# VectorE's and ScalarE's orders written out by name in a hybrid convolution, SSD and FFN block

## The chip, the cores and the metric

The kernel runs on one core of one Trainium2 chip. The metric is device time in microseconds of one execution. Three runs of the kernel before took 1012.22 to 1015.75 us, median 1013.33. A further execution was profiled.

## What is computed

The reference is one block over 512 tokens of width 1024, in float32. Cut to what matters:

```
h = rms_norm(x); proj = h @ w_in          # val | glu | z | x, B, C | dt | gates
conv = silu(layer_norm(conv31(val * sigmoid(glu)))) @ conv_pw   # 31 taps per channel
ssm  = per group of 4 heads: conv4 + silu of x, B, C; chunked scan with
       decay = exp(cumsum(dt * a)); y * silu(z); rms_norm; @ ssm_out_w
x = x + rms_norm((sigmoid(gate0) * conv + sigmoid(gate1) * ssm) @ w_out)
f = (silu(h2 @ w_gate) * (h2 @ w_up)) @ w_down;  out = x + rms_norm(f)
```

There are 8 groups of heads in the scan, numbered 0 to 7 here as in the code, and 31 taps for each of 8 strips of 128 channels.

## The kernel before

[...] A weight strip of 128 x 1024 is loaded as raw by SyncE, ScalarE casts it to whi (L209), and the low part wlo is made either by VectorE as raw minus whi (L216) or by ScalarE writing minus whi (L213) to which a GpSimd DMA adds the raw strip (L214). Each product is three matmuls, high by high, low by high and high by low (`mm3`, L253 to L259).

The run goes through these stages. First the projections of the convolution branch, val and glu, 8 strips each, with the token norm made beside them. Then the groups 0 to 7 of the scan: in each, TensorE makes px (two strips), pB and pC; ScalarE's first tap and VectorE's three further taps of a short convolution (L606, L608) and ScalarE's Silu (L612) make x, B, C. One group behind, `s1` to `s4` work on the group before: transposes pxT (L674), xdt, y and xdec on VectorE, the decay table L, which ScalarE makes with 16 Exps of 128 x 128 per group (L503) and VectorE multiplies with pcb (L693), states (pS, prev), outputs (pY, yo), the product of y with z (L747), four squares jk with row sums (L752), a scale of y (L755), transposes pyT and from them the high and low part yh and yl (L769, L770), which the output projection pso reads. In groups 2, 4 and 6 TensorE also makes pz for that group and the next one, in four banks of tokens, and ScalarE empties each bank by two Silus, zb and z (L658, L659). The 31 taps of the long convolution (L518 for the first, on ScalarE, L521 for the other 30, on VectorE, tiles a0 to a7) are put between these steps. Then come the gates, the layer norm, the pointwise convolution in seven products of half the size (pwx, pwv), the mixing of both branches into pd and its high and low parts m0h, m0l, m1h, m1l (L1054 to L1061), the output projection tm_wo with weights whi, wlo, chi, clo, the residual, gate-up and the down projection.

What sets the order: a scheduler places each engine's instructions in order of the code, with dependences and with extra edges that the kernel adds without any wait on the chip. `not_before` adds such an edge; `by_table` chains all Exps and Silus of ScalarE (and late Sigmoids) in the order of the code; `conv_some` ties each tap to the last matmul emitted; `issue_after` and `keep_in_program_order` do the like for TensorE and SyncE; from the residual on, two tables ORDER_DVE and ORDER_ACT of noted names fix VectorE and ScalarE in gate-up. ScalarE computes Exp, Silu and Sigmoid from tables; where the next function needs another set, the build puts a table load ahead of it (ACT_TABLE_LOAD in the rows).

Of the kernel before, what the change touches and what calls it, by code (L numbers as in the profile page):

```python
# [10 lines left out]
F32 = mybir.dt.float32  # L11
# [7 lines left out]
P = 128  # L19
T = 512  # L20
# [39 lines left out]
for _n, _c in PRM:  # L60
# [30 lines left out]
ADD_S1 = (3, 5)  # L91
ORDER_DVE = (
# [19 lines left out]
).split()  # L112
ORDER_ACT = (
# [62 lines left out]

@with_exitstack
def block_kernel(ctx: ExitStack, tc: tile.TileContext, x, xT, x0, prm, hp, gp, wf, w, out):
    nc = tc.nc
    act, dve, pe, pool = nc.scalar, nc.vector, nc.tensor, nc.gpsimd  # L180
# [14 lines left out]
    def w_raw(n):  # L195
        if n < len(ORDER) and n not in raws:
            if more_raw and n >= GU[0] and n % 7 < 2:
                raws[n] = more_raw[0].tile([P, 1024], F32, tag="raw2", bufs=2, name=f"raw{n}")
            else:
                raws[n] = wp.tile([P, 1024], F32, tag="raw", bufs=RAW_BUFS, name=f"raw{n}")  # L200
            tc.keep_in_program_order(nc.sync.dma_start(raws[n], w[n]))

    def w_part(n, c, by_dve=False):
        hi, lo = split[n]
        src = first_raw[n, c.start] if n < 3 else raws[n][:, c]
        if by_dve:
            dve.tensor_copy(hi[:, c], src)
        else:
            mark[n, c.start] = act.copy(hi[:, c], src)  # L209
        after_zz = n > 5 and ORDER[n - 2] in ZZ_LAST  # L210
        every = n % DMA_EVERY == DMA_EVERY - 1 and DMA_FROM < n < seq[("gc", 0)] and not after_zz
        if every or 0 <= n - seq[("wo", 0)] < ADD_WO:
            act.activation(lo[:, c], hi[:, c].bitcast(F32), AF.Copy, scale=-1.0)  # L213
            mark["lo"] = pool.dma_start(lo[:, c], w[n][:, c].bitcast(F32R), accum_op=ALU.add)  # L214
        else:
            mark["wlo"] = dve.tensor_tensor(out=lo[:, c], in0=src, in1=hi[:, c].bitcast(F32), op=ALU.subtract)  # L216
            if ORDER[n] == ZZ_LAST[0]:
                not_before(noted["yz_1"], mark["wlo"])
# [19 lines left out]
    noted = {}  # L238
# [3 lines left out]
    def note(name, ins):  # L242
        noted[name] = ins
        return ins

    def not_before(ins, first):

        edge = mybir.DependencyInfo(mybir.DependencyClass.NoSync, mybir.DependencyReason.DATA)
        tc.add_manual_dep(ins.ins, first.ins.name, edge, reason="spread")

    def mm3(ps, lh, ll, rh, rl, start, stop, more=False, cut=None):

        mark["pe"] = pe.matmul(ps, lh, rh, start=start, stop=False, skip_group_check=more)  # L253
# [5 lines left out]
        mark["pe3"] = pe.matmul(ps, ll, rh, start=False, stop=stop, skip_group_check=more)  # L259
        return mark["pe"]  # L260

    def power(out_, in_, mul, add, n):
# [3 lines left out]
        mark["pow"] = pool.tensor_tensor(out=out_, in0=m, in1=neg_half[:, :n], op=ALU.pow)  # L266
# [65 lines left out]
    def in_order(ins):  # L332
        return tc.keep_in_program_order(ins)

# [5 lines left out]
    for _ in range(WARM):  # L340
        in_order(pe.matmul(ps[:, :P], woken, woken, start=True, stop=True))
# [15 lines left out]
    def load(c):  # L357
        c = slice(3 * c.start, 3 * c.stop)
        in_order(nc.sync.dma_start(w3[:, c], wf[:, c]))

    for k in range(NK):
        in_order(nc.sync.dma_start(xk[k] if k else x0g[:, : T + NK], xT[k] if k else x0))
# [3 lines left out]
    in_order(nc.sync.dma_start(prm_t, prm))  # L366
    hp_t = ssd.tile([P, 3, H], F32, name="hp_t")
    in_order(nc.sync.dma_start(hp_t, hp))
# [4 lines left out]
    def split_x(k):  # L373
        e_ = dve.scalar_tensor_tensor(
            out=elo[k], in0=xk[k], scalar=pre_g[:, k : k + 1], in1=ehi[k].bitcast(F32), op0=ALU.mult, op1=ALU.subtract,
        )
        if k in parts:
            not_before(e_, mark["wlo"])
# [3 lines left out]
    for k in range(NK):  # L382
        e_ = act.activation(ehi[k], xk[k], AF.Copy, scale=pre_g[:, k : k + 1])
        if k == 4:
            x_split = e_
# [9 lines left out]
    not_before(act.activation(ssq, xk[0], AF.Square), x_split)  # L395
    for k in range(1, NK):
        sq = va_tile(f"sq{k}")
        not_before(act.activation(sq, xk[k], AF.Square), mark[2, 2 * P])
# [16 lines left out]
    def norm_to_all():  # L415
        ps = aux_tile("prb")
        with tc.issue_after(mark["pe"].ins):
            for t in range(NT):
                pe.matmul(ps[:, t * P : (t + 1) * P], ones, dgs[t], start=True, stop=True)
# [45 lines left out]
    def running_sums():  # L465
# [13 lines left out]
        for c in range(NT):  # L479
            nc.scalar.dma_start(scr[:, c, :], acsT[c * H : (c + 1) * H, :])  # L480
# [1317 lines left out]
```

## Time and profile before

| what | us |
|---|---|
| median of three runs | 1013.33 |
| the profiled execution | 1013.44 |
| its span, first to last instruction | 1011.7 |
| TensorE busy | 1003.7 |
| VectorE busy | 845.7 |
| ScalarE busy | 619.8 |
| GpSimd busy | 105.9 |

A profile is one execution, so a sum is made against 1013.44, of which 1.7 us lie outside the span. Rows of the timeline give the start and the duration of an instruction; two instructions of one engine overlap a little, so that the step from start to start is what a further one costs. The waits say which engine stood still for whom. Names are those of the program, with buffer numbers left out.

### The profile page before, as it was taken

The numbers are of one execution on the slowest core, as the hardware profiler recorded it, in microseconds if no ns is written. First come the engines' busy times: TensorE is split into PE (matmuls) and PEld (weight loads), VectorE is DVE, ScalarE is ACT, GpSimd is POOL, SyncE is SP. The second block draws the span as 40 slices with busy tenths as digits, with TensorE's granted clock in tenths as the row PEclk, the third lists the DMA queues.
The fourth block names the chain that finished last, engine by engine and source line by source line (L and its number), as shares of the span: only waits on it lengthen the run. The fifth ranks groups of instructions, "written<-read, shape, count | busy, mean of one in ns | idle before, by whom it ended". The sixth has DMA issues, their size and how long they took to land.

```text
span 1011.7 us, 15883 instructions
## 1 busy us (share of the span) xinstructions
PE 1003.7 (99%) x6152; PEld 877.9 (87%) x6152; DVE 845.7 (84%) x1230; ACT 619.8 (61%) x1045; POOL 105.9 (10%) x138
## 2 busy tenths in 40 slices
PE   9999999999999999999999999999999999999997
PEld 7898889888888888888888889889999999998886
DVE  7899977868696779668987889779999897899984
ACT  7655774767665756573542586487666566668552
POOL 0101202020121011100110110011000000001001
PEclk9999999999999999999999999999999999999999
DMA  8567545645654466356452356734655455459622
GB/s 303 150 167 218 160 100 147 178 111 145 152 165 109 118 190 167 79 144 174 104 126 84 105 122 191 227 115 127 221 147 167 146 147 146 138 172 289 214 84 83
DMA packets 43803, 155.02 MB, mean 153 GB/s; under 512 B 5072, under 2 KB 6096, under 8 KB 42704
## 3 DMA queue, kind: packets, MB, share of 16 engines
q1 hardware_dynamic: 30672, 105.44, 30.6%
q0 software_dynamic: 11136, 43.00, 21.5%
q10 hardware_dynamic: 1920, 5.57, 1.6%
q8 instruction: 48, 0.79, 0.3%
q14 instruction: 27, 0.22, 0.1%
HBM read 149.73 MB, written 4.26 MB: 152 GB/s over the span
## 4 chain that ended last, share of the span: by engine, by line
PE 92%; DVE 4%; ACT 3%; issue 1%; POOL 0%; POOLq 0%; DVEq 0%; ACTq 0%
PE xy L259 4%; PE xy L253 4%; PE xy L255 4%; PE pso L253 3%; PE pso L255 3%; PE pso L259 3%; PE yv L259 2%; PE yv L253 2%; PE yv L255 2%; PE pz L255 2%; PE pz L259 2%; PE pz L253 2%; PE px L259 2%; PE px L253 2%; PE px L255 2%; PE pgs L259 1%
## 5 line engine op out<-in xcount | busy, mean ns | idle before, releaser
L521 DVE SCALAR_TENSOR_TENSOR a<-v,prm_t,a 128x511 f32<-128x511 f32 (+15 forms) x240 | 182.8, 765 | 14.9 <-ACT a L518 12.9
L209 ACT CAST whi<-raw 128x1024 fp32r<-128x1024 f32 x99 | 102.6, 1048 | 127.9 <-PE pso L255 36.7
L216 DVE TENSOR_TENSOR wlo<-raw,whi 128x1024 fp32r<-128x1024 f32 x58 | 70.5, 1218 | 32.9 <-ACT whi L209 32.7
L214 POOL DMA_DIRECT2D wlo<-in_w x41 | 36.5, 889 | 368.8 <-ACT wlo L213 164.5
L255 PE MATMUL pz<-wlo,hhi 128*128 128x512 f32 (+2 forms) x160 | 56.2, 351 | 0.0
L259 PE MATMUL pz<-whi,hlo 128*128 128x512 f32 (+2 forms) x160 | 56.1, 352 | 0.0
L253 PE MATMUL pz<-whi,hhi 128*128 128x512 f32 (+2 forms) x160 | 55.4, 352 | 0.0
L253 PE MATMUL px<-hhi,whi 128*128 128x512 f32 x128 | 50.2, 392 | 0.0
L253 PE MATMUL pso<-yh,whi 128*128 128x512 f32 x128 | 50.2, 395 | 0.0
L1197 ACT CAST whi_g<-raw 128x1024 fp32r<-128x1024 f32 x40 | 41.4, 1051 | 13.9 <-DVE raw L1230 7.7
L259 PE MATMUL px<-hhi,wlo 128*128 128x512 f32 x128 | 49.8, 389 | 0.0
L255 PE MATMUL px<-hlo,whi 128*128 128x512 f32 x128 | 49.8, 389 | 0.0
L255 PE MATMUL pso<-yl,whi 128*128 128x512 f32 x128 | 49.8, 390 | 0.0
L259 PE MATMUL pso<-yh,wlo 128*128 128x512 f32 x128 | 49.7, 390 | 0.0
L608 DVE SCALAR_TENSOR_TENSOR x<-px,prm_t,x 128x511 f32<-128x511 f32 (+2 forms) x48 | 34.7, 742 | 13.8 <-ACT x L606 13.8
L1202 DVE TENSOR_TENSOR wlo_g<-raw,whi_g 128x1024 fp32r<-128x1024 f32 x34 | 41.2, 1219 | 3.6 <-ACT whi_g L1197 3.6
L213 ACT ACTIVATE wlo<-whi 128x1024 fp32r<-128x1024 f32 x41 | 43.3, 1056 | 0.3
L503 ACT ACTIVATE L<-L,nacs 128x128 f32<-128x128 f32 x128 | 38.8, 389 | 1.0 <-POOL L L496 0.9
L255 PEld LDWEIGHTS pz<-wlo,hhi 128*128 128x128 f32 x160 | 30.1, 188 | 4.5 <-DVE wlo L216 0.8
L253 PEld LDWEIGHTS pz<-whi,hhi 128*128 128x128 f32 x160 | 30.2, 189 | 3.8
L259 PEld LDWEIGHTS pz<-whi,hlo 128*128 128x128 f32 x160 | 30.2, 189 | 3.7
L1197 ACT CAST chi_g<-raw 128x1024 fp32r<-128x1024 f32 x24 | 24.9, 1054 | 10.2 <-DVE raw L1230 3.4
(767 smaller groups left out, 3445.2 us busy)
## 6 DMA issues: line engine op xcount, KB each, us to landing
raw<-in_w SPq DMA_DIRECT2D x182, 512.0 KB, 4.5
wlo<-in_w POOLq DMA_DIRECT2D x41, 512.0 KB, 6.9
L<-scr POOLq DMA_DIRECT2D x8, 1024.0 KB, 8.0
wlo_g<-in_w POOLq DMA_DIRECT2D x11, 512.0 KB, 7.6
clo_g<-in_w POOLq DMA_DIRECT2D x6, 512.0 KB, 5.7
pws<-in_w POOLq DMA_DIRECT2D x8, 256.0 KB, 6.0
pw_raws<-in_w SPq DMA_DIRECT2D x4, 512.0 KB, 6.4
xr<-in_x ACTq DMA_DIRECT2D x4, 512.0 KB, 4.2
```

What stands on the lines that cost most here:

```text
L209: mark[n, c.start] = act.copy(hi[:, c], src)
L213: act.activation(lo[:, c], hi[:, c].bitcast(F32), AF.Copy, scale=-1.0)
L214: mark["lo"] = pool.dma_start(lo[:, c], w[n][:, c].bitcast(F32R), accum_op=ALU.add)
L216: mark["wlo"] = dve.tensor_tensor(out=lo[:, c], in0=src, in1=hi[:, c].bitcast(F32), op=ALU.subtract)
L253: mark["pe"] = pe.matmul(ps, lh, rh, start=start, stop=False, skip_group_check=more)
L255: pe.matmul(ps, lh, rl, start=False, stop=False, skip_group_check=more)
L259: mark["pe3"] = pe.matmul(ps, ll, rh, start=False, stop=stop, skip_group_check=more)
L503: act.activation(L[:, h, c, :], L[:, h, c, :], AF.Exp, bias=nacs[:, c, HG * g + h : HG * g + h + 1])
L521: return dve.scalar_tensor_tensor(out=va[j][:, d:], in0=vs[j][:, : T - d], scalar=col("dw_w", j * KC + KC - 1 - d), in1=va[j][:, d:], op0= ...
L608: dve.scalar_tensor_tensor(out=a[:, d:], in0=ps[:, : T - d], scalar=col("ssm_w", i * KS + KS - 1 - d), in1=a[:, d:], op0=ALU.mult, op1=ALU ...
L1197: a_ = act.copy(hi, src)
L1202: d_ = dve.tensor_tensor(out=lo, in0=src, in1=hi.bitcast(F32), op=ALU.subtract)
```

## The change

The extra edges (`not_before`, `by_table`, `note`, `issue_after`, `keep_in_program_order`) are taken out everywhere. At the end of the kernel, five tables give each engine its whole order: VectorE, ScalarE, GpSimd and SyncE by the name of the tile that an instruction writes and a running number, TensorE by ranges of numbers in the order of the code. A new function ties each instruction to the one before it in its table. The instructions themselves, their tiles, shapes and buffers stay the same.

```
+ORDER_ACT = (
...
+    "L5.8 L5.9 zb4_0.0 z4.0 zb4_0.1 z4.1 L5.10 zb4_1.0 whi_54.0 z4.2 whi_55.0 whi_56.0 L5.11 whi_57.0 wlo_55.0 "
...
+ORDER_PE = (
+    "0-680 716-720 681-683 721-724 684-715 725-741 743-753 742 754-925 961-964 969 926-928 970-974 929-960 975-992 "
...
+def in_written_order(nc, tc, orders):
+
+    edge = mybir.DependencyInfo(mybir.DependencyClass.NoSync, mybir.DependencyReason.DATA)
+    made, count = {e: {} for e in orders}, {}
+    for ins in nc.cur_bb.bb.instructions:
+        if ins.engine in made and ins.outs and hasattr(ins.outs[0], "bass_ap"):
+            name = ins.outs[0].bass_ap.tensor.name.rpartition("_")[0]
+            n = count[ins.engine, name] = count.get((ins.engine, name), -1) + 1
+            made[ins.engine][f"{name}.{n}"] = ins
+    for engine, order in orders.items():
+        names = list(made[engine])
+        if order[0][0].isdigit():
+            spans = [[int(i) for i in span.split("-")] for span in order]
+            order = [names[i] for span in spans for i in range(span[0], span[-1] + 1)]
+        assert sorted(order) == sorted(names)
+        for first, then in zip(order, order[1:]):
+            tc.add_manual_dep(made[engine][then], made[engine][first].name, edge, reason="order")
...
-    def by_table(ins):
-
-        if "table" in mark:
-            not_before(ins, mark["table"])
-        mark["table"] = ins
-
-    def make_L(g, first=None):
+    def make_L(g):
...
-                by_table(
-                    act.activation(L[:, h, c, :], L[:, h, c, :], AF.Exp, bias=nacs[:, c, HG * g + h : HG * g + h + 1])
-                )
+                act.activation(L[:, h, c, :], L[:, h, c, :], AF.Exp, bias=nacs[:, c, HG * g + h : HG * g + h + 1])
...
-            not_before(taps.pop(0)(), mark["pe"])
+            taps.pop(0)()
...
+    orders = ORDER_ACT, ORDER_DVE, ORDER_PE, ORDER_POOL, ORDER_SP
+    in_written_order(nc, tc, {q.engine: order for q, order in zip((act, dve, pe, pool, sync), orders)})
```

What the tables move is seen in the built orders. First place: ScalarE from the squares of group 3 (jk, with row sums in ss3) to the first banks of pz of group 4, which zb4 and z4 empty; y3 is the scale behind the squares. Before:

```order
L612 ACTIVATE C4_2829<-C4_2829 128x512
L752 ACTIVATE jk_2849,ss3_2847<-y3_2657 128x256
L752 ACTIVATE jk_2851,ss3_2847<-y3_2657 128x256
L213 ACTIVATE wlo_53_2880<-whi_53_2879 128x1024
L752 ACTIVATE jk_2853,ss3_2847<-y3_2657 128x256
L752 ACTIVATE jk_2855,ss3_2847<-y3_2657 128x256
L658 ACTIVATE zb4_0_2869<-pz4_0_2884 128x256
L659 ACTIVATE z4_2868<-pz4_0_2884 128x256
L755 ACTIVATE y3_2657<-y3_2657,rs3_2848 128x256 x4
L658 ACTIVATE zb4_0_2869<-pz4_1_2911 128x256
L659 ACTIVATE z4_2868<-pz4_1_2911 128x256
```

And now:

```order
L889 ACTIVATE jk_2855,ss3_2847<-y3_2657 128x256
L643 ACTIVATE L5_3018<-L5_3018,nacs_234 128x128
L750 ACT_TABLE_LOAD
L750 ACTIVATE C4_2829<-C4_2829 128x512
L892 ACTIVATE y3_2657<-y3_2657,rs3_2848 128x256 x4
L643 ACT_TABLE_LOAD
L643 ACTIVATE L5_3018<-L5_3018,nacs_234 128x128 x8
L795 ACT_TABLE_LOAD
L795 ACTIVATE zb4_0_2869<-pz4_0_2884 128x256
L796 ACTIVATE z4_2868<-pz4_0_2884 128x256
L795 ACTIVATE zb4_0_2869<-pz4_1_2911 128x256
L796 ACTIVATE z4_2868<-pz4_1_2911 128x256
```

C4's Silu, the scale and eight Exps of group 5 now stand ahead of the first zb and z, with three table loads.

Second place: the same engine to the end of that stretch, where the last bank of pz of group 4 is emptied and x5, the first strip of group 5, and yh2, the high part of y of group 3, follow. Before:

```order
L209 CAST whi_57_3011<-raw57_2984 128x1024
L658 ACTIVATE zb4_1_2870<-pz4_3_2965 128x256
L213 ACTIVATE wlo_57_3012<-whi_57_3011 128x1024
L659 ACTIVATE z4_2868<-pz4_3_2965 128x256
L503 ACT_TABLE_LOAD
L503 ACTIVATE L5_3018<-L5_3018,nacs_234 128x128 x16
L606 ACTIVATE x5_0_3068<-px5_0_3043,prm_t_75 128x512
L209 CAST whi_58_3161<-raw58_2997 128x1024
L518 ACTIVATE a5_3154<-v5_881,prm_t_75 128x512
L606 ACTIVATE x5_1_3099<-px5_1_3074,prm_t_75 128x512
L769 ACTIVATE yh2_2777<-pyT3_0_3105,prm_t_75 128x512
```

And now:

```order
L379 CAST whi_57_3011<-raw57_2984 128x1024
L383 ACTIVATE wlo_55_2987<-whi_55_2986 128x1024
L795 ACT_TABLE_LOAD
L795 ACTIVATE zb4_1_2870<-pz4_3_2965 128x256
L796 ACTIVATE z4_2868<-pz4_3_2965 128x256
L383 ACTIVATE wlo_57_3012<-whi_57_3011 128x1024
L744 ACTIVATE x5_0_3068<-px5_0_3043,prm_t_75 128x512
L379 CAST whi_58_3161<-raw58_2997 128x1024
L643 ACT_TABLE_LOAD
L643 ACTIVATE L5_3018<-L5_3018,nacs_234 128x128 x4
L750 ACT_TABLE_LOAD
L750 ACTIVATE x5_0_3068<-x5_0_3068 128x512
```

The 16 Exps are in pieces of 2, 8, 1, 1 and 4 between other steps; yh2 follows right behind the last row. From the first jk to that yh2 there are nine table loads now and there was one.

Third place: VectorE ahead of the output projection, whose low parts of the weights are clo_108 to clo_110 and wlo_111, wlo_112. Before:

```order
L1058 TENSOR_TENSOR m0l_5345<-pd3_1_5640,m0h_5344 128x256
L1058 TENSOR_TENSOR m1l_5347<-pd3_1_5640,m1h_5346 128x256
L216 TENSOR_TENSOR clo_108_5890<-raw108_5763,chi_108_5889 128x1024
L216 TENSOR_TENSOR clo_109_5896<-raw109_5795,chi_109_5895 128x1024
L216 TENSOR_TENSOR clo_110_5902<-raw110_5887,chi_110_5901 128x1024
L216 TENSOR_TENSOR wlo_111_5908<-raw111_5893,whi_111_5907 128x1024
L216 TENSOR_TENSOR wlo_112_5914<-raw112_5899,whi_112_5913 128x1024
```

And now, beginning with the second of eleven mixing steps behind clo_108:

```order
L1172 TENSOR_TENSOR m1l_5347<-pd1_0_5388,m1h_5346 128x256
L1172 TENSOR_TENSOR m1l_5347<-pd0_1_5352,m1h_5346 128x256
L1175 SCALAR_TENSOR_TENSOR pd3_1_5640<-pwx3_5637,prm_t_75,gc7_5305 128x256
L1194 TENSOR_TENSOR pd3_0_5639<-pwv3_5638,pd3_0_5639 128x256
L1175 SCALAR_TENSOR_TENSOR pd3_0_5639<-pd3_0_5639,prm_t_75,gc6_5271 128x512
L1172 TENSOR_TENSOR m0l_5345<-pd1_1_5389,m0h_5344 128x256
L1168 TENSOR_TENSOR pd3_0_5639<-so6_1100,pd3_0_5639 128x512
L1172 TENSOR_TENSOR m0l_5345<-pd2_0_5514,m0h_5344 128x256
L1175 SCALAR_TENSOR_TENSOR pd3_1_5640<-pd3_1_5640,prm_t_75,gc7_5305 128x256
L1168 TENSOR_TENSOR pd3_1_5640<-so7_1101,pd3_1_5640 128x512
L386 TENSOR_TENSOR wlo_111_5908<-raw111_5893,whi_111_5907 128x1024
L386 TENSOR_TENSOR clo_109_5896<-raw109_5795,chi_109_5895 128x1024
```

The mixing steps that stood ahead of clo_108 now stand between it and clo_109, and wlo_111 has moved ahead of clo_109. Behind clo_109 follow an m1l, clo_110, two m0l, wlo_112, three m1l and the last m0l.

More of the change, by code (lines that the diff above doesn't have):

```diff
@@ L237, in block_kernel @@
     mark = {}
-    noted = {}
     first_raw = {}
     hlo = None
[L242 to L249, printed above, removed]
     def mm3(ps, lh, ll, rh, rl, start, stop, more=False, cut=None):
-        mark["pe"] = pe.matmul(ps, lh, rh, start=start, stop=False, skip_group_check=more)
+        pe.matmul(ps, lh, rh, start=start, stop=False, skip_group_check=more)
         if cut is None:
@@ L258, in mm3 @@
                 pe.matmul(ps[:, c], lh, rl[:, c], start=False, stop=False, skip_group_check=True)
-        mark["pe3"] = pe.matmul(ps, ll, rh, start=False, stop=stop, skip_group_check=more)
-        return mark["pe"]
+        pe.matmul(ps, ll, rh, start=False, stop=stop, skip_group_check=more)
     def power(out_, in_, mul, add, n):
@@ L340, in block_kernel @@
     for _ in range(WARM):
-        in_order(pe.matmul(ps[:, :P], woken, woken, start=True, stop=True))
+        pe.matmul(ps[:, :P], woken, woken, start=True, stop=True)
     x0g = ssd.tile([P, 3 * GW], F32, tag="yo", name="x0g")
@@ L416, in norm_to_all @@
         ps = aux_tile("prb")
-        with tc.issue_after(mark["pe"].ins):
-            for t in range(NT):
-                pe.matmul(ps[:, t * P : (t + 1) * P], ones, dgs[t], start=True, stop=True)
+        for t in range(NT):
+            pe.matmul(ps[:, t * P : (t + 1) * P], ones, dgs[t], start=True, stop=True)
         act.copy(rb, ps)
@@ L834, in gate @@
             proj(ps, w_get(n, i))
-        mark["gate"] = act.activation(out_, ps, AF.Sigmoid, bias=col("gate_b", i + (NK if n == "gs" else 0)))
+        act.activation(out_, ps, AF.Sigmoid, bias=col("gate_b", i + (NK if n == "gs" else 0)))
         gates[n, i] = out_
@@ L875, in ln_mean @@
         ps = aux_tile("plm")
-        with tc.issue_after(mark["pe"].ins):
-            pe.matmul(ps, ones, vsum, start=True, stop=True)
+        pe.matmul(ps, ones, vsum, start=True, stop=True)
         return ps
@@ L888, in ln_factor @@
         ps = aux_tile("plv")
-        with tc.issue_after(mark["pe"].ins):
-            for t in range(NT):
-                pe.matmul(ps[:, t : t + 1], sqsum[:, t * P : (t + 1) * P], ones[:, :1], start=True, stop=True)
+        for t in range(NT):
+            pe.matmul(ps[:, t : t + 1], sqsum[:, t * P : (t + 1) * P], ones[:, :1], start=True, stop=True)
         act.copy(lrs, ps[:, :NT])
@@ L1009, in block_kernel @@
         if i == LN_ALL:
-            first_ = act.activation(warm, warm, AF.Silu)
-            not_before(first_, mark["gate"])
-            by_table(first_)
+            act.activation(warm, warm, AF.Silu)
             ln_all()
@@ L1037, in pw_product @@
             cut = CUT if (u, wn, k) in CUT_PW else None
-            m = mm3(ps, wh[:, c], wl[:, c], mh[:, k], ml[:, k], start and k == 0, k == K2 - 1, not start, cut)
-            if k == 0:
-                not_before(m, before)
+            mm3(ps, wh[:, c], wl[:, c], mh[:, k], ml[:, k], start and k == 0, k == K2 - 1, not start, cut)
     def pw_first(u):
@@ L1254, in product @@
             cut = CUT if (u, wn, k) in CUT_GU else None
-            m = mm3(ps, wh[:, c], wl[:, c], mh[:, k], ml[:, k], start and k == 0, k == KB - 1, not start, cut)
-            if k == 0 and mark.get("chain"):
-                not_before(m, last)
+            mm3(ps, wh[:, c], wl[:, c], mh[:, k], ml[:, k], start and k == 0, k == KB - 1, not start, cut)
     xrs, xgs = {}, {}
@@ L1466, in v2 @@
         product(V[u], u, "s4", "b22", False)
-        note(f"v2_{u}", add(d[:, c2], V[u]))
+        add(d[:, c2], V[u])
         if e == 0:
-            note(f"si2_{u}", act.activation(d, d, AF.Silu))
+            act.activation(d, d, AF.Silu)
         else:
-            note(f"g2_{u}", dve.tensor_tensor(out=d, in0=d, in1=sg[f][0], op=ALU.mult))
+            dve.tensor_tensor(out=d, in0=d, in1=sg[f][0], op=ALU.mult)
     def x4(u):
```

280 lines of the change are left out of this document (107 added, 173 removed), and 215 rows, old and new, of tables (ORDER_ACT, ORDER_DVE, ORDER_PE, ORDER_POOL).

## The prediction

> **What bounds the kernel now.** I read the page first, for the engines' shares and the chain that ended last, then what TensorE waited for, then stretches of the run, and last the rows of ScalarE and VectorE in the two places where the order changes most. The page's rows on TensorE:
>
> ```profile
> PE 1003.7 (99%) x6152; PEld 877.9 (87%) x6152; DVE 845.7 (84%) x1230; ACT 619.8 (61%) x1045; POOL 105.9 (10%) x138
> PE 92%; DVE 4%; ACT 3%; issue 1%; POOL 0%; POOLq 0%; DVEq 0%; ACTq 0%
> ```
>
> TensorE is busy for 1003.7 of 1011.7 us, and 92% of the chain that ended last are its own matmuls. All that it waited for on other engines stands in three rows of the waits (engine and line, for whom, us in total, times, longest):
>
> ```profile
> PE warm_ps L341 <- DVE woken L336: 1.0, 1, 1.0
> PE pxT L674 <- DVE yl L770: 0.4, 1, 0.4
> PE ptr L1306 <- ACT mg L1290: 0.2, 1, 0.2
> ```
>
> The first is the start of the program, which the change leaves alone. So 0.6 us is all that better placed steps can win on TensorE: nothing here is 0.3% of the run (3.0 us, about what a measurement of this kernel can tell from no change). The matmuls are the same 5793 in both programs, in the same order but for one transpose, so a gain over 3 us has no place to come from. What can happen is that TensorE begins to wait. Once it does, it does not catch up, as the table by stretches shows (busy time of each engine):
>
> ```profile
> 150.00:312.00 162.00, 161.63 (x1016) 136.66 (x1016) 129.42 (x181) 98.70 (x185) 24.88 (x26) 1.00 0.53 144
> 312.00:345.00 33.00, 33.00 (x160) 27.29 (x159) 18.62 (x26) 27.15 (x56) 3.92 (x5) 1.00 0.54 143
> 345.00:600.00 255.00, 255.00 (x1387) 211.48 (x1386) 209.49 (x294) 139.70 (x229) 29.95 (x35) 1.00 0.46 122
> 600.00:656.00 56.00, 55.96 (x411) 52.33 (x410) 48.85 (x77) 30.22 (x50) 3.84 (x5) 1.00 0.71 214
> ```
>
> From 312 to 656 us TensorE (the third number) has 0.04 us of idle time to give back. I therefore speak of its lag: how much later a matmul starts than in the profile shown. Two late steps in parallel count once, with the larger lag; only a lag that starts from TensorE's own late result adds.
>
> **The change part by part: what is equal.** SyncE's order is the same row for row. GpSimd's differs in a few places (two memsets, the masks of three groups against their neighbours, one load), on an engine that is busy 10%. From the first residual (656 us) to the end VectorE's and ScalarE's orders are the same too, so gate-up, down projection and tail keep their times and only start later. On VectorE nothing is added: it is its 1229 instructions in another order. On ScalarE there is an addition that the diff does not show: the built order has 57 table loads where it had 28. The old program tied every Exp, Silu and (late) Sigmoid of that engine into one chain in program order, which kept 16 Exps of a group behind one load; the new order spreads them as filling, so Exp and Silu take turns.
>
> **The price of a load.** ScalarE's rows around the Exps of group 5 (start, duration, line, tiles, count):
>
> ```profile
> 313.36 0.42 ACT L752 ACTIVATE jk<-y 128x256 f32<-128x256 f32 x1 [4.12 <-DVE y L747]
> 314.32 1.04 ACT L213 ACTIVATE wlo<-whi 128x1024 fp32r<-128x1024 f32 x1
> 315.27 0.40 ACT L752 ACTIVATE jk<-y 128x256 f32<-128x256 f32 x1
> 316.62 0.38 ACT L658 ACTIVATE zb<-pz 128x256 f32<-128x256 f32 x1 [0.32 <-PE pz L259]
> 316.90 0.38 ACT L659 ACTIVATE z<-pz 128x256 f32<-128x256 f32 x1
> 328.13 0.37 ACT L659 ACTIVATE z<-pz 128x256 f32<-128x256 f32 x1
> 328.52 1.28 ACT L503 ACT_TABLE_LOAD   x1
> 329.81 4.79 ACT L503 ACTIVATE L<-L,nacs 128x128 f32<-128x128 f32 x16
> 334.51 0.76 ACT L606 ACTIVATE x<-px,prm_t 128x512 f32<-128x512 f32 x1
> 336.11 0.82 ACT L518 ACTIVATE a<-v,prm_t 128x512 f32<-128x512 f32 x1
> 336.83 0.76 ACT L606 ACTIVATE x<-px,prm_t 128x512 f32<-128x512 f32 x1
> 337.50 1.25 ACT L769 ACTIVATE yh<-pyT,prm_t 128x512 fp32r<-128x512 f32 x2
> 340.41 0.63 ACT L612 ACTIVATE x<-x 128x512 f32<-128x512 f32 x1
> 340.95 1.04 ACT L209 CAST whi<-raw 128x1024 fp32r<-128x1024 f32 x1
> ```
>
> Without a load, z starts 0.28 us after zb (316.62 to 316.90). With a load between, the first Exp starts 1.68 us after z (328.13 to 329.81). A load thus costs 1.40 us: 1.29 of its own, and the overlap of two instructions that is lost. Over the run 29 more come to 40.6 us, which the share hides (619.8 would become 660, still 65%). It counts where ScalarE is near its limit, and that is one stage: between 312 and 345 us it is busy 27.15 of 33.00 us.
>
> [...]
>
> **First term: the z stage of group 4.** The order quoted above has nine loads between the first square (jk) of group 3 and the scaled cast yh of that group, where before it had one. Behind each load wait, on ScalarE, the zb and z that empty the banks in which TensorE puts the next pz, and yh. In the same way the stretches of groups 2 and 6 get five and seven loads for one each, so I work out the worst. ScalarE in that stretch of the old run:
>
> ```profile
> 313.36:337.50 24.14, 24.14 (x113) 19.82 (x112) 9.76 (x13) 21.91 (x49) 3.92 (x5) 1.00 0.67 174
> ```
>
> It is busy 21.91 of 24.14 us: 2.23 us are free. The new order puts in 8 loads more, 11.20 us, and two Silus that stood outside (C and x, 0.54 each by 340.41 to 340.95), 1.08. It takes out a wlo (314.32 to 315.27, 0.95), the first tap a (336.11 to 336.83, 0.72), an x (0.67) and one Exp (4.70 over 16, 0.29), 2.63 together. Net 9.65 us; if all 2.23 free us are filled, yh comes 7.42 us later than its 337.50, counted from the same start. The start, VectorE's product y that the squares wait for, and the end, the step yl behind yh and the matmul behind that:
>
> ```profile
> 311.47 0.72 DVE L521 SCALAR_TENSOR_TENSOR a<-v,prm_t,a 128x493 f32<-128x493 f32 x1
> 312.12 1.21 DVE L747 TENSOR_TENSOR y<-y,z 128x1024 f32<-128x1024 f32 x1
> 339.21 0.74 DVE L770 SCALAR_TENSOR_TENSOR yl<-pyT,prm_t,yh 128x512 fp32r<-128x512 f32 x1
> 340.06 0.61 PE L674 MATMUL pxT<-ident,x 128*128 128x128 f32 x4
> 303.00 0.59 PE L728 MATMUL pYb<-prev,C 128*128 128x256 f32 x2
> ```
>
> In the new order no tap stands right ahead of y: the start is 0.65 us earlier (311.47 to 312.12). At the end yl ran at 339.21, though its yh was done at 338.17 (337.50 and one cast of 0.67): 1.04 us of cover, because two steps of x stood ahead. pxT started 0.11 us after yl ended, so beyond that there is no cover. TensorE's lag is 7.42 - 0.65 - 1.04 = **5.7 us**. The uncertain part is the start. Earliest, y can follow TensorE's pYb (ends 303.59) by two steps and itself, some 6.5 us before its old time, and the lag would be zero. But the new order puts 28 more taps and one more wlo ahead of it on VectorE and takes three C steps away: 28 x 0.65 + 1.14 - 3 x 0.65 = 17.4 us, of the 32.6 us that VectorE had free from 150 to 312. Latest, it moves with TensorE's own lag from the z stage of group 2. I take the old time less 0.65, because free time and added work are both large and neither clearly wins.
>
> **Second term: the way into the output projection.** Before, the low parts of wo (clo) follow each other and all mixing steps stand ahead of them. Now eleven mixing steps and a wlo stand between the first clo and the second. VectorE's steps there in the old run, and the matmuls that matter:
>
> ```profile
> 635.92 0.48 DVE L1061 SCALAR_TENSOR_TENSOR pd<-pwx,prm_t,gc 128x256 f32<-128x256 f32 x1
> 636.31 1.21 DVE L216 TENSOR_TENSOR wlo<-raw,whi 128x1024 fp32r<-128x1024 f32 x1
> 637.45 0.42 DVE L1058 TENSOR_TENSOR m0l<-pd,m0h 128x256 fp32r<-128x256 f32 x1
> 637.78 0.42 DVE L1058 TENSOR_TENSOR m1l<-pd,m1h 128x256 fp32r<-128x256 f32 x1
> 638.12 0.68 DVE L1054 TENSOR_TENSOR pd<-so,pd 128x512 f32<-128x512 f32 x1
> 638.72 1.22 DVE L216 TENSOR_TENSOR wlo<-raw,whi 128x1024 fp32r<-128x1024 f32 x1
> 642.43 0.28 PE L259 MATMUL pwx<-v_t4h,wlo_C 128*128 128x256 f32 x1
> 651.61 0.39 PE L253 MATMUL tm_wo<-chi,m0h 128*128 128x512 f32 x1
> 651.84 0.39 PE L255 MATMUL tm_wo<-clo,m0h 128*128 128x512 f32 x1
> 656.14 0.39 PE L259 MATMUL tm_wo<-whi,m0l 128*128 128x512 f32 x1
> ```
>
> Steps by these rows: 0.39 (pd of 256), 1.14 (wlo or clo), 0.33 (m0l, m1l), 0.60 (pd of 512). The cast chi ahead of clo waits for TensorE's last pwx (ends 642.71) and takes 1.05, so clo can start at 643.8. To the second clo: 1.14 + 4 x 0.60 + 2 x 0.39 + 5 x 0.33 + 1.14 = 7.1, so it starts at 650.9 and ends at 652.1, where tm_wo wants it at 651.84: 0.3 late. To the last m0l: two clo and a wlo (3.42), six small steps (1.98) and its own 0.42, 656.7, wanted at 656.14: 0.6 late. Since it starts from TensorE, this **0.6 us** adds (bounds: 0, if the casts run ahead, and 1.2, double).
>
> Elsewhere the order brings VectorE's steps late by less: in group 1, 18 taps more and 10 fewer, with a wlo more, stand ahead of xdec, 6.3 us of work. It counts once, under the 5.7.
>
> **The sum.** The profiled execution took 1013.44 us with a span of 1011.7, and the median shown is 1013.33. 1013.44 + 5.7 + 0.6 = 1019.7 us. The terms' bounds: four tap steps either way at the start (2.6), 0.6 either way in the second, so 1016.5 to 1022.9.
>
> **The rivals.** (1) *The cover holds*: the three C steps that now stand behind y let VectorE reach it earlier, and ScalarE's loads fall into idle time. At the earliest start only the 0.6 us is left, 1014.0 us. It decides from a start of y before 308.2, 3.3 us ahead of the one taken: then the whole lag is under 3.0 us, no measurable change. For it speaks the free VectorE time, against it the 28 taps ahead. (2) *The lags add*: y in group 3 is held by TensorE's own lateness from group 2, so that the stretch of group 4 adds its 5.7 to a lag of the same kind: 1025.4. Five loads for one there make 5.6 us, so the size is right; against it speaks that y has 6.5 us between pYb and its old time. (3) *A cold clock*: the waits come in one piece long enough for the granted clock to fall. An early product of the run, in the chain:
>
> ```profile
> 5.06 0.43 PE pv L573
> ```
>
> It held the engine for 0.43 us, against 0.23 for the same shape in the rows above (651.61 to 651.84); ten such steps cost 2 us, two such falls bring 1023.7. The trace shows no long wait in mid-run. [...]
>
> **How the numbers follow.** Forecast 0.63; (1) 0.15; (2) 0.10; (3) 0.06; (4) 0.04; anything else, a gain included, 0.02. Slower by over 0.3% (above 1016.4) are the forecast, (2), (3) and (4): 0.83. Within 0.3%: 0.15. Faster: 0.02. The range leaves out (4), the rest and most of (1): 1015.5 to 1026.0.
>
> **What would show it.** Right: 57 table loads at 1.28 us; TensorE's waits of several us in all between 180 and 345 us, ended by ScalarE's z or VectorE's yl and xdec, a lag of 5 to 6 us at pxT of group 4, and under 1 us more by 656 us, with clo or m0l as releaser; the same duration from there to the end. Wrong: pxT of group 4 near 340 us (rival 1), a lag that grows again at groups 5 to 7 (rival 2), or waits in gate-up.

## The result and the profile after

The changed kernel takes 1025.82 us, the median of four runs (1023.89 to 1026.22); the kernel before, run beside it, 1013.01 (1012.22 to 1015.75). The ratio is 1.0118, interval 1.0095 to 1.0141: slower, just inside the range on record (0.2 us below its upper end), and by twice the forecast step (12.8 us for 6.3). The profiled execution is the fastest of the four, 1023.89 us with a span of 1022.0, so what follows accounts for 10.3 us of span.

From the page of the changed kernel, the busy time of each engine:

```profile
span 1022.0 us, 15935 instructions
PE 1006.3 (98%) x6152; PEld 878.6 (86%) x6152; DVE 854.3 (84%) x1230; ACT 659.4 (65%) x1074; POOL 113.1 (11%) x138
```

ScalarE is busy 39.6 us more (40.6 were worked out) with 29 instructions more, all table loads. From the groups by line, the two largest groups of loads, at the Exps of L and at the Silus of x, B and C; before they were 8 and 8:

```profile
L643 ACT ACT_TABLE_LOAD x22 | 28.2, 1283 | 0.3
L750 ACT ACT_TABLE_LOAD x13 | 16.7, 1283 | 6.1 <-DVE x L746 5.9
```

The waits of TensorE, of which before had 1.0, 0.4 and 0.2:

```profile
PE pz L411 <- ACT z L796: 5.0, 3, 2.9
...
PE pSa L841 <- DVE xdec L819: 0.9, 1, 0.9
PE pxT L811 <- DVE yl L907: 0.8, 1, 0.8
PE tm_wo L413 <- DVE clo L386: 0.7, 1, 0.7
PE pz L411 <- DVE C L746: 0.5, 1, 0.5
```

Where in the run the time is lost is read from steps that both kernels have. The timeline of before at the last pYb of group 1, and that of the changed kernel at six steps of TensorE whose old times stand in the prediction (303.00, 340.06, 631.81 in the row below, 642.43, 651.84):

```profile
202.47 0.59 PE L728 MATMUL pYb<-prev,C 128*128 128x256 f32 x2
631.81 1.08 PE L253 MATMUL tm_wo<-whi,m0h 128*128 128x512 f32 x4
```

```profile
204.20 0.59 PE L865 MATMUL pYb<-prev,C 128*128 128x256 f32 x2
308.99 0.59 PE L865 MATMUL pYb<-prev,C 128*128 128x256 f32 x2
349.32 0.66 PE L811 MATMUL pxT<-ident,x 128*128 128x128 f32 x4 [0.80 <-DVE yl L907]
641.32 1.08 PE L411 MATMUL tm_wo<-whi,m0h 128*128 128x512 f32 x4
651.51 0.28 PE L417 MATMUL pwx<-v_t4h,wlo_C 128*128 128x256 f32 x1
661.77 0.50 PE L413 MATMUL tm_wo<-clo,m0h 128*128 128x512 f32 x1 [0.69 <-DVE clo L386]
```

TensorE's lag is 1.73 us at group 1's pYb, 5.99 at group 3's, 9.26 at pxT of group 4, 10.12 at a pYb behind the wait of group 6 (479.77 before, 489.89 now), 9.51 at the first product of the output projection, 9.08 where the mixing stage ends, 9.93 at clo_109, 10.3 at the end. So it has lost 1.7 us by the first scans (the wait at pSa the most of it), 4.3 more by group 3 (that is in group 2), 3.3 in group 4 and 0.9 in group 6, where the third wait for z, of 0.47 us, stands. The stretch from there to the end of the mixing stage gives 1.0 back, and the projection takes 1.2.

The largest piece is group 2. TensorE at its last pz, and ScalarE, which empties the bank:

```profile
220.91 0.54 PE L411 MATMUL pz<-whi,hhi 128*128 128x512 f32 x1 [2.93 <-ACT z L796]
221.25 0.62 PE L413 MATMUL pz<-wlo,hhi 128*128 128x512 f32 x1
221.67 0.63 PE L417 MATMUL pz<-whi,hlo 128*128 128x512 f32 x1
224.66 0.40 PE L411 MATMUL pz<-whi,hhi 128*128 128x512 f32 x1
211.92 0.42 ACT L889 ACTIVATE jk<-y 128x256 f32<-128x256 f32 x1
217.64 1.26 ACT L643 ACTIVATE L<-L,nacs 128x128 f32<-128x128 f32 x4
218.91 1.28 ACT L795 ACT_TABLE_LOAD   x1
220.20 0.38 ACT L795 ACTIVATE zb<-pz 128x256 f32<-128x256 f32 x1
220.48 0.38 ACT L796 ACTIVATE z<-pz 128x256 f32<-128x256 f32 x1
```

From the first square (211.92) to the first zb it is 8.28 us: four squares, ten Exps, the scaling and a load. After the wait a matmul takes 0.63 us, for 0.39 in the rows of before (651.61). The windows of that place, the first with most of the wait and the second right behind it, with the granted clock in the column behind GpSimd's:

```profile
217.83:221.24 3.41, 0.48 (x2) 0.30 (x2) 3.41 (x6) 3.39 (x9) 0.00 (x0) 1.00 0.00 0
221.24:224.65 3.41, 3.41 (x9) 2.66 (x8) 2.12 (x4) 3.35 (x5) 0.00 (x0) 0.50 0.00 0
```

The clock fell to 0.50 for 3.41 us: half of that, 1.7 us, is the estimate of what comes on top of the wait. By the rows eight matmuls start between 221.25 and 224.66, 0.43 us apart, against 0.23 before (651.61 to 651.84): 1.6 us in all.

At group 4, where the prediction put its first term, the steps that it used (old times 312.12, 337.50, 339.21, 340.06):

```profile
315.09 1.23 DVE L884 TENSOR_TENSOR y<-y,z 128x1024 f32<-128x1024 f32 x1
347.81 1.25 ACT L906 ACTIVATE yh<-pyT,prm_t 128x512 fp32r<-128x512 f32 x2
348.51 0.75 DVE L907 SCALAR_TENSOR_TENSOR yl<-pyT,prm_t,yh 128x512 fp32r<-128x512 f32 x1 [2.60 <-ACT yh L906]
```

The product y starts 2.97 us later than before, yh 10.31 later. TensorE's pYb of this group, from which y is made, comes 5.99 us later, so y has moved 3.02 us nearer to it: 6.10 us behind it now (315.09 - 308.99), 9.12 before (312.12 - 303.00).

### The profile page after: what moved, and what is told of

It is laid out like the page before. It is cut to its first block, busy times and chain, and to the rows that moved or that the text cites. A ratio compares the mean times of both kernels' runs of the same rounds, so it can differ in the third digit from the quotient of the medians.

```text
span 1022.0 us, 15935 instructions
## 1 busy us (share of the span) xinstructions
PE 1006.3 (98%) x6152; PEld 878.6 (86%) x6152; DVE 854.3 (84%) x1230; ACT 659.4 (65%) x1074; POOL 113.1 (11%) x138
## 4 chain that ended last, share of the span: by engine, by line
PE 55%; ACT 1%; DVE 1%; issue 0%; POOL 0%; POOLq 0%; DVEq 0%; ACTq 0%
PE xy L411 4%; PE xy L417 4%; PE xy L413 4%; PE yv L411 2%; PE yv L413 2%; PE yv L417 2%; PE pgs L417 1%; PE pgc L411 1%; PE pgs L413 1%; PE pgs L411 1%; PE pso L411 1%; PE pso L417 1%; PE pgc L413 1%; PE pgc L417 1%; PE pso L413 1%; PE tm_a L413 1%
## 5 line engine op out<-in xcount | busy, mean ns | idle before, releaser
L660 DVE SCALAR_TENSOR_TENSOR a<-v,prm_t,a 128x511 f32<-128x511 f32 (+17 forms) x240 | 174.2, 772 | 5.5 <-ACT a L657 4.4
L643 ACT ACTIVATE L<-L,nacs 128x128 f32<-128x128 f32 x128 | 41.5, 390 | 1.5 <-POOL L L637 1.2
```

Of the source, the lines that this page charges most:

```text
L643: act.activation(L[:, h, c, :], L[:, h, c, :], AF.Exp, bias=nacs[:, c, HG * g + h : HG * g + h + 1])
L660: return dve.scalar_tensor_tensor(out=va[j][:, d:], in0=vs[j][:, : T - d], scalar=col("dw_w", j * KC + KC - 1 - d), in1=va[j][:, d:], op0= ...
```

## The experiments

The theory to test: ScalarE's stretch from y to z and to yh became too long, by Exps and their loads, and y follows TensorE, so that what one group loses is there for the next. Its rivals: the position of the Exps alone, VectorE's order alone, or a stretch whose loss is absorbed later.

### Loads taken out, order kept

```
-                act.activation(L[:, h, c, :], L[:, h, c, :], AF.Exp, bias=nacs[...])
+                act.activation(L[:, h, c, :], L[:, h, c, :], AF.Silu, bias=nacs[...])
```

> The changed kernel with Silu in place of Exp in the decay matrix L (so L is a different matrix), every instruction in the same place: ScalarE then stays on one table through the groups, and 37 of the 57 table loads go. Theory 'loads' (the lateness is the added loads): the wait before the last pz of group 2 falls from 2.93 us to about 1.6 (one load of 1.28 stands between the squares and zb), too short for the low clock after it, and the waits of groups 4 (1.57, and 0.80 at pxT) and 6 (0.47) go: about 6 us less than the changed kernel, near 1019.5. Rival 'position' (the Exps and the scaling ahead of zb and z hold the bank, whatever the table): the waits stay within 0.3 us each and the time stays near 1025.

Measured: 1019.53 us, ratio 1.0057 (1.0042 to 1.0072). The only z wait that is left, in the timeline of this run, is that of group 2:

```profile
219.77 0.50 PE L411 MATMUL pz<-whi,hhi 128*128 128x512 f32 x1 [1.54 <-ACT z L796]
```

The wait is 2.93 - 1.54 = 1.39 us shorter, one load's price by the rows of before (1.40), the clock stays up (the matmuls behind the wait take 0.39 to 0.40 us, for 0.63), and groups 4 and 6 no longer wait for z or yl. So 6.3 of the 12.8 us come from the loads, and the waits account for them: 1.39, the 1.7 estimated for the clock, and the old 1.57, 0.80 and 0.47 are 5.9 us. "Position" alone falls. What is left in group 2 is Exps ahead of zb, without a load.

### The zs put first

```
-... jk.7 L3.4 ... L3.9 y1.0 y1.1 y1.2 y1.3 L3.10 ... L3.13 zb2_0.0 z2.0 zb2_0.1 z2.1 L3.14 ...
+... jk.7 zb2_0.0 z2.0 zb2_0.1 z2.1 L3.4 ... L3.9 y1.0 y1.1 y1.2 y1.3 L3.10 ... L3.14 ...
```

and so in groups 4 (behind jk.15) and 6 (behind jk.23).

> The changed kernel with the first two zb and z of groups 2, 4 and 6 put right behind the squares, ahead of the scaling and the Exps; 55 loads for 57. Theory 'position': the z waits of groups 2, 4 and 6 (2.93, 1.57, 0.47) and the low clock of 1.7 us go, while yh of group 4 stands behind as many loads as before, so the 0.80 us at pxT stays or grows by up to the 1.9 us that group 4 gains: 1018 to 1020. Rival 'loads': with 55 loads left, the waits only move to the next step that TensorE needs (the second zb and z, yh), and the time stays above 1023.

Measured: 1035.43 us, ratio 1.0218 (1.0201 to 1.0236), 9.6 us more than the changed kernel. The waits for z are gone, and these came, in the waits of this run:

```profile
PE pxT L811 <- DVE yl L907: 8.5, 3, 3.9
PE pB L417 <- DMA wlo<-in_w: 3.5, 1, 3.5
PE pSa L841 <- DVE xdec L819: 2.1, 2, 1.5
```

The theory of position falls. Zs taken first push the scaling, and with it yh, yl and pxT, behind the same loads, and a low part of a weight, which comes by way of ScalarE and a GpSimd DMA, landed 3.5 us too late for pB. The granted clock falls to 0.50 twice besides, for 6.83 and 3.41 us. The rival foresaw that the waits move; that the time rises was in neither expectation.

### VectorE's taps put behind y

```
-... xdec1.0 ... a3.18 ... a2.19 ... a3.19 a2.20 a3.20 a2.21 ... a3.21 ... a2.22 ... y1.5 ...
+... xdec1.0 ... y1.5 a3.18 a2.19 a3.19 a2.20 a3.20 a2.21 a3.21 a2.22 ...
```

and so in groups 3 (5 taps) and 5 (4 taps).

> The changed kernel with the 8, 5 and 4 tap steps that VectorE has between xdec and the last product y of groups 1, 3 and 5 put behind that product; ScalarE's order and its 57 loads are untouched. Theory 'start' (the ScalarE stretch is late because VectorE's y starts it late): y and the squares start up to 8 x 0.65 = 5.2, 3.3 and 2.6 us earlier, and the z waits of groups 2, 4, 6 and the low clock go: 1018 to 1020. Rival 'length' (ScalarE's stretch is bound by TensorE's results, not by y): the squares start less than 1 us earlier and the time stays above 1023.

Measured: 1020.28 us, ratio 1.0072 (1.0057 to 1.0087). TensorE's last pYb and VectorE's y of group 3:

```profile
306.08 0.59 PE L865 MATMUL pYb<-prev,C 128*128 128x256 f32 x2
309.41 1.23 DVE L884 TENSOR_TENSOR y<-y,z 128x1024 f32<-128x1024 f32 x1
```

In the changed kernel y starts 6.10 us behind pYb, here 3.33. The waits for z of groups 2 and 4 are gone, and so is the low clock (a mean of 0.998 over the span, for 0.997), as "start" has it, and "length" falls; the wait of group 6 stays (0.8 us), and so does the one at pxT (0.8). The 5.5 us won and the 6.3 of the loads are for the most part the same waits, ended once by an earlier start and once by a shorter stretch, so they should not add. No run has both, so that is not shown.

### Two steps of VectorE moved at the other waits

```
-... xdt1.0 xdt1.1 y1.1 L1.0 xdec1.0 ...        ... pd3_1.3 wlo_111.0 clo_109.0 ... wlo_112.0 ... m0l.7
+... xdt1.0 xdt1.1 xdec1.0 y1.1 L1.0 ...        ... pd3_1.3 clo_109.0 ... m0l.7 wlo_111.0 wlo_112.0
```

> The changed kernel with VectorE's xdec of group 1 put ahead of the product L, and wlo_111 and wlo_112 put behind the last m0l; nothing else moved. Both theories: the waits at pSa (0.91) and at tm_wo (0.69) go. Theory 'given back' (y of group 1 is set by VectorE's own unbroken row of work): TensorE reaches the last pz of group 2 about 1.5 us earlier and waits there 4.4 us for 2.93, so only the 1.2 us at the output projection stay, 1 to 1.5 us less than the changed kernel. Rival 'adds': both stay, 2.5 to 3 us less.

Measured: 1025.62 us, ratio 1.0119 (1.0104 to 1.0134), the changed kernel's time. Both expectations miss, since each wait only took another name:

```profile
PE pz L411 <- ACT z L796: 5.6, 3, 2.9
PE tm_wo L413 <- DVE wlo L386: 1.4, 1, 1.4
PE pSb L841 <- DVE y L815: 1.3, 1, 1.3
```

VectorE has more to do ahead of these matmuls than time: in the changed kernel it is busy for 59.86 of the 60 us from 140 to 200. xdec is early and y, which stood behind it, is late for pSb; clo_109 is early and wlo_111, wanted a few matmuls on, is late by 1.4 us.

### The Exps together, as before

ORDER_ACT with the 16 Exps of L3, L5 and L7 behind z2.3, z4.3 and z6.3, written short:

```
-... L3.0 L3.1 L3.2 L3.3 jk.4 ... L3.4 ... zb2_0.0 ... z2.3 L3.15 a4.0 x3_0.0 ...
+... jk.4 ... zb2_0.0 ... z2.3 L3.0 ... L3.15 a4.0 x3_0.0 ...
```

> The changed kernel with the 16 Exps each of L3, L5 and L7 put together behind the last z of groups 2, 4 and 6, where the kernel before has them; VectorE's order untouched; 39 table loads for 57. Theory 'chain' (squares to z on ScalarE is too long by Exps and loads together): from the squares to the first zb only the scaling and one load are left, the z waits of groups 2, 4, 6 (2.93, 1.57, 0.47) and the low clock (1.7) go, pxT of group 4 (0.80) goes or halves: 8 to 9 us less than the changed kernel, 1017 to 1018, and the waits at the first scans and at the output projection stay. Rival 'moved': as in the run with z put ahead, yh of groups 2, 4, 6 now stands behind 16 Exps in one piece, and pxT waits 2 us and more each: above 1022.

Measured: 1027.98 us, ratio 1.0141 (1.0124 to 1.0158). The rival "moved" was right. The wait at pxT in this run, and rows of ScalarE's timeline from the Exps of L3 to yh:

```profile
PE pxT L811 <- DVE yl L907: 7.2, 3, 3.0
```

```profile
230.84 4.79 ACT L643 ACTIVATE L<-L,nacs 128x128 f32<-128x128 f32 x16
237.84 0.82 ACT L657 ACTIVATE a<-v,prm_t 128x512 f32<-128x512 f32 x1
239.43 1.28 ACT L750 ACT_TABLE_LOAD   x1 [0.78 <-DVE x L746]
241.92 1.25 ACT L906 ACTIVATE yh<-pyT,prm_t 128x512 fp32r<-128x512 f32 x2
```

The kernel before has its Exps here too. But the written order also puts two first taps and the Silu of x3 with its load ahead of yh, with 0.78 us of waiting for VectorE's x. Eighteen loads fewer did not help: by the order, what else stands ahead of yh has stayed, and the Exps have joined it. No run moves those other steps alone. The intervals of this run and of the changed kernel overlap, so that it is slower is not shown; that nothing was won is.

### Both remedies

The order of ScalarE of the run before and that of VectorE with the taps behind y:

```
+ORDER_ACT: ... z2.3 L3.0 ... L3.15 a4.0 x3_0.0 ...
+ORDER_DVE: ... y1.5 a3.18 a2.19 ... a2.22 ...
```

> The run before this one with, besides, VectorE's 8, 5 and 4 taps put behind the last product y of groups 1, 3 and 5. Theory 'chain': the early start and the short stretch are two ways of paying the same wait, so with both the time is within 1.5 us of the one with the Exps together. Rival 'two costs' (the start and the length each cost on their own): 4 to 5.5 us less than with the Exps together, that is 1012 to 1013.5.

Measured: 1028.67 us, ratio 1.0139 (1.0119 to 1.0158), within 1.5 us of the one without the taps. The waits at pxT are 7.2 us again. "Two costs" falls: in an order where pxT waits for yh in every one of these groups, an early y is worth nothing.

### The old order up to the layer norm, the new one behind

```
-ORDER_ACT: (new) ... whi_A0.0 gc3.0 | vf.0 vf.1 ... (new)
+ORDER_ACT: (old, 551 steps)        | vf.0 vf.1 ... (new)
-ORDER_DVE: (new) ... wlo_93.0 so7.3 | a0.30 a1.30 ... (new)
+ORDER_DVE: (old, 666 steps)        | a0.30 a1.30 ... (new)
```

> The orders of ScalarE, VectorE, GpSimd, SyncE and TensorE of the kernel before written out up to the end of the groups and the convolution, and ScalarE's and VectorE's of the changed kernel from there (the mixing steps and the way into the output projection); 28 loads. Theory: the mixing stage gives about 1.0 us (TensorE's lag falls from 10.1 to 9.1 us there) and the output projection takes 1.2 to 1.3 back: 1013 to 1014.5, no measurable change. Rival: the loss at the projection shows only because TensorE comes early after the mixing stage, so that both cancel exactly, or the projection loses more when the lag is gone: 1015 and above.

Measured: 1014.12 us, ratio 1.0006 (0.9996 to 1.0015), no change. The old wait at pxT and the new one at the projection stand side by side:

```profile
PE tm_wo L413 <- DVE clo L386: 0.7, 1, 0.7
PE pxT L811 <- DVE yl L907: 0.4, 1, 0.4
```

So the convolution and the groups hold the whole loss, and the stretch from the layer norm on none that can be measured.

### ScalarE's spread Exps in the old order

All orders of before written out, with ScalarE's jk, Exps, scaling, zb and z of groups 2, 4 and 6 in the order of the changed kernel:

```
-... jk.4 zb2_0.0 jk.5 z2.0 jk.6 zb2_0.1 jk.7 z2.1 y1.0 y1.1 y1.2 y1.3 zb2_1.0 ... z2.3 L3.0 ... L3.15 ...
+... L3.0 ... L3.3 jk.4 jk.5 jk.6 jk.7 L3.4 ... L3.9 y1.0 ... L3.13 zb2_0.0 z2.0 zb2_0.1 z2.1 L3.14 ... z2.3 L3.15 ...
```

> The orders of the kernel before written out on all engines, with ScalarE alone changed between the squares and the last z of groups 2, 4 and 6: there the Exps of L3, L5 and L7, the scaling and the zb and z stand as in the changed kernel; 42 table loads for 28, VectorE untouched. Theory 'chain': in the changed kernel it is 8.3 us from the first square to the first zb of group 2, and here the squares start at 212.8 us, so z comes at 221.6 where TensorE wants the bank at 216.3: a wait of about 5 us and 1.7 us of low clock, and 3 to 5 us in groups 4 and 6 each: 1024 to 1031, so that ScalarE's order alone is enough for the whole loss. Rival 'taps': the loss comes from VectorE's order and ScalarE's alone costs under 4 us: below 1017.5.

Measured: 1032.15 us, ratio 1.0187 (1.0167 to 1.0207), a little above the range, with these waits for z, and the window behind the first of them:

```profile
PE pz L411 <- ACT z L796: 11.8, 3, 4.9
```

```profile
220.26:227.09 6.83, 6.01 (x14) 4.81 (x15) 1.13 (x1) 6.08 (x11) 0.00 (x0) 0.50 0.00 0
```

The wait of group 2, the longest, is the 5 us worked out, and the granted clock at its end is 0.50 for 6.83 us; behind the waits of groups 4 and 6 (2.80 and 4.11 us) it is 0.50 for 3.41 us each. So of the loss 11.8 us are waits and, by estimate, 6.8 the clock (half of the 13.65 us at 0.50). ScalarE's order alone is enough for more than the whole loss. VectorE's then takes some of it back, it seems, by bringing y nearer to pYb, and costs the first scans their 1.7 us, since there is no wait at pSa here; no run has VectorE's new order alone, so its share is not shown.

TensorE's last pYb and VectorE's y of group 3 in this run, where VectorE's order is the old one:

```profile
310.13 0.59 PE L865 MATMUL pYb<-prev,C 128*128 128x256 f32 x2
319.17 1.22 DVE L884 TENSOR_TENSOR y<-y,z 128x1024 f32<-128x1024 f32 x1
```

TensorE is 7.13 us late at pYb and y 7.05: y stands 9.04 us behind pYb, for 9.12 before. So in the old order, too, y had no time of its own; it followed TensorE.

### Loads taken out in one group

```
+                    L[:, h, c, :], L[:, h, c, :], AF.Silu if g == 3 else AF.Exp, bias=nacs[...]
```

> The changed kernel with Silu in place of Exp in L3 alone (so L3 is a different matrix); 51 table loads for 57, all orders as in the changed kernel. Theory 'lags add' (VectorE's last product y of a group comes a fixed 5.5 us behind TensorE's last pYb, whatever TensorE's lag): the loss in group 2 falls from 4.8 us to about 1.6 (as with all loads off), and groups 4 and 6 lose what they lost before (z 0.46 and 1.57, pxT 0.80, z 0.47): 3 us less than the changed kernel, near 1022.5. Rival 'absorbed' (y of group 3 stands at a time of its own, as the prediction took it): what group 2 loses less, group 4 loses more; its z wait and pxT grow by about 3 us together and the time stays near 1025.

Measured: 1022.39 us, ratio 1.0085 (1.0070 to 1.0101). TensorE's waits for z and at pxT, and in the timeline its last pYb, VectorE's y of group 3 and pxT of group 4:

```profile
PE pz L411 <- ACT z L798: 3.6, 3, 1.6
PE pxT L813 <- DVE yl L909: 0.8, 1, 0.8
```

```profile
307.20 0.59 PE L867 MATMUL pYb<-prev,C 128*128 128x256 f32 x2
313.25 1.22 DVE L886 TENSOR_TENSOR y<-y,z 128x1024 f32<-128x1024 f32 x1
347.49 0.66 PE L813 MATMUL pxT<-ident,x 128*128 128x128 f32 x4 [0.76 <-DVE yl L909]
```

TensorE is 1.79 us earlier at pYb than in the changed kernel, though the first scans cost 1.2 us more in this execution (pYb of group 1 at 205.41 for 204.20), and y comes 6.05 us behind it (6.10 there): it follows TensorE. Group 4 adds the same on top: from pYb to pxT the lag grows by 7.43 - 4.20 = 3.23 us here, by 9.26 - 5.99 = 3.27 in the changed kernel, with the same waits for z and at pxT, 1.6 and 0.8. The lags add, and "absorbed" falls.

### Three small moves in the old order

```
 ORDER_ACT, old:  -x3_1.0 yh0.2 yh0.3 x3_0.1
                  +yh0.2 yh0.3 x3_1.0 x3_0.1
 ORDER_DVE, old:  -x3_0.2 x3_1.0 yl0.2 x3_1.1
                  +x3_0.2 yl0.2 x3_1.0 x3_1.1
                  -wlo_s1.0 pd1_0.2 pd1_1.2 pd1_0.3 wlo_C2.0
                  +wlo_s1.0 wlo_C2.0 pd1_0.2 pd1_1.2 pd1_0.3
                  -pd2_0.1 pd2_1.1 pd2_0.2 wlo_C3.0
                  +pd2_0.1 wlo_C3.0 pd2_1.1 pd2_0.2
```

> The orders of the kernel before written out on all engines, with three moves: ScalarE's start of x3_1 behind yh0.3 and VectorE's yl0.2 ahead of its first step on x3_1 (for the wait of 0.37 us at pxT of group 2), and VectorE's wlo_C2 and wlo_C3 two and three steps earlier (for the slow row of matmuls at 628.7 to 629.4 us). Theory: pxT's wait goes (0.57 us with the slow matmul behind it) and 0.2 to 0.5 us of the mixing stage: 0.6 to 1.0 us less than the kernel before, ratio 0.9990 to 0.9994. Rival: another step takes the place of each, and the ratio is 1.000 or above.

Measured: 1012.98 us, ratio 0.9997 (0.9987 to 1.0007) (medians of 11 and 15 executions). The wait at pxT is gone, the span is 1010.9 us for 1011.7, and one wait is new in the mixing stage:

```profile
PE pwx L411 <- DVE pd L1188: 0.2, 1, 0.2
```

The time is not measurably other than that of before. With TensorE 99% busy, these moves win nothing that the times show.

## Why the prediction was right in sign and too small

**The bound and the loads.** TensorE bounds the kernel, the loads are 57, each 1.28 us, and the price of 1.40 taken for one is what the run with the loads out showed (1.39). The chance of 0.04 under (4) stood for a load at about twice this price. No run shows such a price: one load less on the way to zb made TensorE's wait there 1.39 us shorter.

**The first term.** The stretch was sized well and its start was not. From y to yh it grew by 10.31 - 2.97 = 7.34 us; 7.42 was worked out. The step that failed is "I take the old time less 0.65" for y. y came 2.97 us later than its old time, and 7.42 + 2.97 - 1.04 = 9.35 is what TensorE's lag at pxT then should be; 9.26 was measured. In a given order y keeps its distance from TensorE's pYb: in group 3 9.12 us before and 9.04 in the old order with TensorE 7.13 us late, 6.10 in the changed kernel and 6.05 with the lag made shorter. So the 6.5 us that the text saw between pYb and y's old time were no reserve against a lag; taps and other steps stand in them ahead of y whatever the time. (Their size was a little high too: with the taps behind y 3.33 us are left of 9.12, which is 5.8.)

The step thus holds two errors of opposite sign. The new order brings y 3.02 us nearer to pYb, where 0.65 was taken: by that group 4 alone costs 7.42 - 3.02 - 1.04 = 3.4 us and not 5.7, and 3.3 was measured. And the 5.99 us that the first scans and group 2 cost came through to y in full, where nothing was taken.

**Groups 1, 2 and 6.** "In the same way" and "it counts once, under the 5.7" were the same error: taking the worst stretch stood for a maximum where the terms add. Group 2, with fewer loads than group 4, cost most, 4.3 us. Ten Exps and the scaling stood ahead of zb there, and its wait of 2.93 us was followed by the low clock. Group 6 added 0.9.

**The second term.** The place and the releaser were right, and the size was 0.85 to clo_109 (9.08 to 9.93), where 0.3 was worked out, and 1.2 with what follows, for 0.6: the upper bound. The cause was as told, mixing steps and wlo_111 ahead of clo_109. Not foreseen was that the stretch ahead of it, up to the end of the mixing stage, gives 1.0 us back; which of its moves does it, the runs do not tell apart.

**The rivals.** The second, "the lags add", is what happened, and it had a chance of 0.10, because of the reserve just told. That its price of 1025.4 is so near the median of 1025.82 is in part luck: it adds 5.7 to 5.7, where 5.99 and 3.3 were measured, and the profiled execution took 1023.89. The median lies inside the range only because the range was drawn wide enough to hold this rival. The third, the cold clock, took part with one fall, where two had been priced, of ten slow steps and 2 us each. The ten were the author's estimate, which no run shows; the changed kernel has eight slow steps in its fall, 1.6 us. The first, that the cover holds, falls. Of the signs named, the loads, the engines that ended the waits and the unchanged stretch behind 656 us came true; the lag of 5 to 6 us at pxT of group 4 did not (9.26), and a lag that grows again in groups 5 to 7, the sign for the second rival, was seen (0.9 us in group 6).

**What stays open.** The median is 1.9 us above the profiled execution. In several profiled executions of the other kernels TensorE waited 1.5 us more for mg in the residual, behind GpSimd's rs_b, and 0.6 us each at the first two scans. That the other executions of the changed kernel hold such waits is likely and not shown.

## What to carry to other kernels

A step that one engine makes from another's result, with filling of its own ahead of it, has no time of its own. Here it stood at a fixed distance behind that result, in group 3 9.0 to 9.1 us in the old order and 6.1 in the new, so lags from separate places add and must be summed, not compared; the time between the result and the step is a reserve only if the filling can move. Work that table loads split into pieces paid for it here, 22 loads of 1.28 us at the Exps of L for 8 before, and stood ahead of a result; yet putting the pieces together again, in an order that was made without them, won nothing here. Where two engines were near their limit (TensorE and VectorE busy for 59.03 and 59.86 of the 60 us from 140 to 200 in the changed kernel), moving one late step ahead of another only renamed the wait, from 0.9 us at pSa to 1.3 at pSb.

## What the runs showed of the hardware

A wait of TensorE cost more than its length: behind the 2.93 us in the changed kernel the granted clock was 0.50 for 3.41 us, 1.6 us more by the rows. In the traces of the kernel before and of the changed kernel the record of the clock begins at 6.07 and 6.20 us. Before, it shows 1.00 from there to 1009.59, behind the last matmul. In the changed kernel a matmul takes 0.63 us ahead of 6.20 (at 5.53) and 0.40 behind it (at 6.31), and the clock is 1.00 up to 221.24, 0.50 up to 224.66 and 1.00 up to 1019.96, again behind the last matmul. These lengths are 294 times 3.413 us before and 63, 1 and 233 times 3.413 us now.

The waits of 1.57 us at z of group 4 in the changed kernel and of 1.54 us at z of group 2 with the loads out had no fall behind them. Length alone did not decide: behind 2.74 us at pxT of group 2 in the run with both remedies the clock was 0.50 from 243.67 on; behind 2.73 us there with the Exps together and 3.03 us there with the zs put first it stayed at 1.00. The runs with 2.74 and 3.03 us differ in how long TensorE stood still within one stretch of 3.41 us, counted from the falls of the same run: 1.87 us with the zs put first, without a fall, and 2.12 us with both remedies, with one. In the changed kernel it is 1.17 us at the wait of 1.57 (327.05 to 330.47), without a fall, and 2.93 us at the wait of 2.93, with one. No more than these four waits was compared in this way; what decides is not shown. First the stretch of the 3.03 us wait (busy 1.54 of 3.41 us), then that of the 2.74 us (busy 1.29) with the one behind it:

```profile
240.83:244.24 3.41, 1.54 (x9) 1.36 (x10) 3.38 (x6) 3.38 (x6) 0.00 (x0) 1.00 0.49 145
```

```profile
240.26:243.67 3.41, 1.29 (x8) 1.17 (x9) 3.38 (x6) 3.38 (x6) 0.00 (x0) 1.00 0.34 137
243.67:247.08 3.41, 3.41 (x10) 2.62 (x9) 3.41 (x3) 1.06 (x3) 0.88 (x1) 0.50 0.83 193
```

The fall lasted 3.41 us in the changed kernel and with both remedies, and 6.83 us at the first of the two with the zs put first and behind the wait of group 2 with the spread Exps.
